# Two mixers and two expert layers in front of a second block: six PSUM banks for the first V pass, row sums in the first mixer, one U block in V

## The chip, the cores and the metric

The kernel runs as one program on one core of a Trainium2 chip. The metric is the device time of one execution in microseconds. The core has five engines that run side by side: TensorE (PE, matmuls; PEld is its weight load), VectorE (DVE), ScalarE (ACT), GpSimd (POOL) and SyncE (SP), which here only issues DMAs.

## What the reference computes

Two blocks of two layers each over 256 tokens of width 1024; the first block also carries 256 context tokens. What matters here is the first block. Each of its layers is a mixer (latent attention, a Fourier branch and a convolution, gated and merged) and then an expert layer with 16384 experts: every token picks 16 experts in each of 8 heads, and

```python
u = jnp.take(u_tab, eid, axis=0)
act = jax.nn.gelu(jnp.einsum('chkd,cd->chk', u, hc)) * gate
v = jnp.take(v_tab, eid, axis=0)
return jnp.einsum('chk,chkd->cd', act, v)
```

Shifts, scales and gates of each layer come from a conditioning row: `silu(cond) @ w_mod + b_mod`, 6 times 1024 numbers for each layer of the first block. The second block is two layers of FFN, hybrid attention, FFN, with conditioning of its own.

## The kernel before, in words

**Numbers.** Every large product is done in three matmuls (`mm3`, lines 369 to 373): weights and activations are split into a high part (rounded to float32r) and a low part, and high x high, high x low and low x high are summed in a PSUM bank. Weights arrive in pieces of 512 KB (128 x 1024, `raw`, issued on SP). `split` makes the high half on ACT (`wh`, line 339) and the low half on DVE (`wl`, line 340; with `share` set, each second or third of them on POOL). There are four `raw` buffers and two each of `wh` and `wl` in the first block's mixers and in its first expert layer.

**The order of the work.** A scheduler puts the instructions of each engine in a fixed order when the kernel is built: it takes them in the order of the program, moves ready ones ahead by simulated times, and `high_priority(300)` lets the top-k work overtake. `issue_after(x)` keeps instructions behind `x` on that engine. On the chip each engine goes through its list and waits where an input or a buffer is not there.

**The mixer** (`mixer`, line 798 on). Its last stage (lines 928 to 968) merges the three branches. For each of eight output blocks d it makes three sums in four `mm` banks, which DVE multiplies with the gates (lines 943 and 947) and splits into `m`; between these d the remaining 18 of 24 gate blocks are computed. Then `wout` is applied for eight d, and DVE adds the result to `xt` (line 961).

**The expert layer** (`peer`, line 1173 on) does not gather for most tokens: it computes all experts densely and zeroes what was not picked. In the first layer 384 of the 512 tokens go this way (nd = 384); the first 128 (g0) are done by row gathers (`rows_up`, `rows_down`), 128 rows each.

- *U stage.* 32 blocks of four steps; each step is one piece of `ut`, 24 matmuls and a Gelu. The block's result `a4` is written to DRAM (`ad`, line 1260). Between the steps `topk` advances by a budget: each of its yields has a cost, a step pays 3.05 of them in the first layer. At its end `topk` writes gate sums from one-hot matmuls (lines 1093 to 1125) to DRAM (`gd`). For the first layer the loop always runs all 32 blocks. `rows_up` advances 1.17 rows a step once the first tile's picks are there.
- *V pass.* `prep` (line 1273) loads gate sums (`g4`) and `a4` of a block, multiplies them on DVE (line 1285) and splits the product into `w4h` and `w4l`. Two blocks form a group (`deep` = 2, so 16 groups): for each of eight d, 8 x 3 matmuls of 384 columns into one `mm` bank, which DVE adds to `xt` in two instructions (line 1292). Behind each of these, `sums` advances by 0.42 steps and `rows_down` by 1.15 rows (DVE line 1170, the gathers on POOL, line 1138, four buffers).
- *Banks.* The layer has 2 `mm` banks, 3 `sc`, 1 `io` and 2 for `xg`, from its beginning to its end.
- *Bias table.* `bias_load` and `bias_write` (lines 1474 to 1498) make a table for the second block; two DMAs of 1532 KB on POOL's queue (`dd`) write it.

**Row sums** (`sums_begin`, `sums_step`, `sums`, `sums_end`, lines 420 to 468). The conditioning of later layers is not made by matmuls: each of its 128-row pieces (512 KB, `arow`) is loaded on SP into a ring and multiplied on DVE with the conditioning row, the product's sum going to one column (line 443). A step issues one load and does the product of the load before (by the ring's depth). For the second layer of the first block there are 48 pieces; the first 16 are needed for both conditioning rows, so they take two products. These 48 run in the first V pass, with a ring of four.

Of the kernel before, what the change touches and what calls it, by code (L numbers as in the profile page):

```python
# [233 lines left out]
class Kernel:  # L234
# [563 lines left out]
    def mixer(self, l):  # L798
# [6 lines left out]
        with ExitStack() as es:  # L805
# [121 lines left out]
            with self.banks(mm=4, sc=3), self.pool(f"op{l}") as op:  # L927
                m = self.t(op, [P, 2, 8, n], "m", F32R)
                v = [self.t(op, [P, 2, n], f"v{j}", F32R) for j in range(2)]
                for cc in range(2):  # L930
                    y, h, lo = st["acc"][:, cc], v[0][:, cc], v[1][:, cc]
                    nc.scalar.activation(h, y, AF.Copy, scale=0.5)
                    nc.vector.scalar_tensor_tensor(lo, y, 0.5, h.bitcast(F32), op0=OP.mult, op1=OP.subtract)
                wb = self.stream("wb", 8 * l)
                for d in range(8):
                    acc = None
                    for b, (act, k0, nk) in enumerate(((st["ao"], 0, 4), (st["f"], 4, 2), (v, 6, 2))):
                        ps = self.ps("mm")[:, :n]
                        for k in range(nk):
                            wh, wl = wb(d * 8 + k0 + k)  # L940
                            self.mm3(ps, wh, wl, act[0][:, k], act[1][:, k], k == 0, k == nk - 1)
                        t = self.t(op, [P, n], "gt" if b == 0 else "gu", bufs=2)
                        nc.vector.scalar_tensor_tensor(t, zg[3 * d + b], 1.0, ps, op0=OP.add, op1=OP.mult)
                        if acc is None:
                            acc = t
                        else:
                            nc.vector.tensor_tensor(acc, acc, t, op=OP.add)
                    nc.scalar.activation(m[:, 0, d], acc, AF.Copy, scale=0.5)
                    nc.vector.scalar_tensor_tensor(
                        m[:, 1, d], acc, 0.5, m[:, 0, d].bitcast(F32), op0=OP.mult, op1=OP.subtract  # L950
                    )
                    self.fill(f)
                    for _ in range(3):
                        i = next(gates, None)
                        if i is not None:
                            gate(i)

                def e3(d, ps):
                    for s in range(len(streams)):
                        x = self.xt[:, d, cols_of(s)]  # L960
                        nc.vector.scalar_tensor_tensor(
                            x, ps[:, cols_of(s)], mod[:, 16 + d, s : s + 1], x, op0=OP.mult, op1=OP.add
                        )
                        self.track(d, s)

                if l == 0:
                    self.need(30)
                self.linear(self.stream("wout", 8 * l), 8, range(8), (lambda k: m[:, 0, k], lambda k: m[:, 1, k]), e3, n=n)

# [8 lines left out]
    rate = {("gate", 0): (10, 0, 2), ("gate", 1): (4, 0, 2), ("u", 0): 0, ("u", 1): 0, ("v", 0): 0.42, ("v", 1): 1.25, "up": 1.17, "down": 1.15, "ffn": 1.4, "out": 1, "att": (0.4, 0.4), "norm": ((4,4), (2,2), (4,4), (4,4))}  # L978
# [194 lines left out]
    def peer(self, l, budget):  # L1173
# [8 lines left out]
        with ExitStack() as es:  # L1182
            es.enter_context(self.banks(mm=2 if g0 else 4, sc=3, io=1))
# [12 lines left out]
            with self.pool(f"tp{l}") as tp:  # L1196
# [44 lines left out]
                while nb < 32 and not (done and not g0):  # L1241
# [25 lines left out]
            if nb == 32:  # L1267
                hes.close()
            with self.pool(f"vp{l}") as vp:
# [52 lines left out]
                if l == 0:  # L1322
                    self.sums_begin(
                        vp, 4, (0, 1), self.sums_of("wmodt", 0, self.mod1[1], "b_mod1", lambda m: (0, 1) if m < 16 else (0,))
                    )
                else:
# [26 lines left out]
                self.sums_end()  # L1353
# [294 lines left out]
    def run(self):  # L1648
# [13 lines left out]
        self.peer(0, 3.05)  # L1662
# [39 lines left out]
```

## Time and profile before

| | |
|---|---|
| median of 3 runs | 4217.4 us (4212.7 to 4218.16) |
| profiled execution | 4220.82 us |
| its span, first to last instruction | 4219.0 us |
| mean granted TensorE clock | 0.946 |
| busy: PE, DVE, ACT, POOL | 3821.8, 3217.7, 1792.4, 959.9 us |
| moved by DMA | 946.53 MB, 224 GB/s |

The stages follow one another on one core: first mixer to about 490 us, first expert layer from there (U stage to 1292, V pass to 1988), second mixer to about 2256, second expert layer to about 3092, then the second block. Times of rows below are counted from the span's first instruction. A line of the profile names engine, line of the kernel, the tile written and the tiles read; the idle time of an engine stands with the instruction that it waited for, and "waits" rows give a total, a count and the longest wait in us. A table of stretches gives for each stretch its length, then busy time (and number of instructions begun) of PE, PEld, DVE, ACT and POOL, the granted TensorE clock, the share of DMA time and GB/s.

### The profile page before, as it was taken

The numbers are of one execution on the slowest core, as the hardware profiler recorded it, in microseconds if no ns is written. First come the engines' busy times: TensorE is split into PE (matmuls) and PEld (weight loads), VectorE is DVE, ScalarE is ACT, GpSimd is POOL, SyncE is SP. The second block draws the span as 40 slices with busy tenths as digits, with TensorE's granted clock in tenths as the row PEclk, the third lists the DMA queues.
The fourth block names the chain that finished last, engine by engine and source line by source line (L and its number), as shares of the span: only waits on it lengthen the run. The fifth ranks groups of instructions, "written<-read, shape, count | busy, mean of one in ns | idle before, by whom it ended". The sixth has DMA issues, their size and how long they took to land.

```text
span 4219.0 us, 69354 instructions
## 1 busy us (share of the span) xinstructions
PE 3821.8 (91%) x25443; PEld 3558.0 (84%) x25443; DVE 3217.7 (76%) x7949; ACT 1792.4 (42%) x2986; POOL 959.9 (23%) x804
## 2 busy tenths in 40 slices
PE   7889998888885789999989999999989989999898
PEld 5568798888884688888778999999989879998798
DVE  4754589999895799997758998788868768656764
ACT  3342332433442222233444656544444554444643
POOL 0100024755543233330201758100000010101100
PEclk9999999999986899999999999999999989999999
DMA  5422257898757999994325777999869429554344
GB/s 179 155 79 97 80 202 275 297 312 281 247 188 170 321 343 351 363 358 152 119 71 180 241 255 241 364 361 358 311 233 316 165 78 323 171 185 150 100 159 142
DMA packets 331412, 946.53 MB, mean 224 GB/s; under 512 B 30865, under 2 KB 118545, under 8 KB 331073
## 3 DMA queue, kind: packets, MB, share of 16 engines
q1 hardware_dynamic: 201920, 722.93, 48.8%
q0 software_dynamic: 38272, 137.38, 10.2%
q10 hardware_dynamic: 90880, 81.79, 5.8%
q8 instruction: 201, 3.29, 0.3%
q14 instruction: 139, 1.13, 0.1%
HBM read 856.01 MB, written 85.98 MB: 223 GB/s over the span
## 4 chain that ended last, share of the span: by engine, by line
PE 37%; DVE 7%; issue 7%; DMA 1%; ACT 1%; POOL 1%; ACTq 0%; POOLq 0%; DVEq 0%; SPq 0%
PE mm L371 11%; PE mm L373 11%; PE mm L372 11%; DVE wl L340 2%; DVE cj L1053 1%; PE sc L1114 1%; DMA raw<-in_vt 1%; ACT wh L339 1%; DVE cacc L770 0%; DVE nu L535 0%; PE sc L510 0%; PE sc L699 0%; PE nm L709 0%; ACTq L1260 0%; PE sc L495 0%
## 5 line engine op out<-in xcount | busy, mean ns | idle before, releaser
L339 ACT ACTIVATE wh<-raw 128x1024 fp32r<-128x1024 f32 x946 | 997.2, 1057 | 1604.9 <-PE mm L372 1254.7
L340 DVE TENSOR_TENSOR wl<-raw,wh 128x1024 fp32r<-128x1024 f32 x839 | 1043.4, 1247 | 502.8 <-ACT wh L339 492.2
L371 PE MATMUL mm<-w4h,wh 128*128 128x384 f32 (+1 forms) x2048 | 642.7, 317 | 95.0 <-DVE xt L1292 53.7
L373 PE MATMUL mm<-h2h,wl 128*128 128x256 f32 (+2 forms) x2176 | 689.3, 318 | 39.3 <-DVE wl L340 37.7
L371 PE MATMUL mm<-h2h,wh 128*128 128x256 f32 (+2 forms) x2176 | 689.4, 318 | 25.6 <-ACT a L1229 16.0
L372 PE MATMUL mm<-h2l,wh 128*128 128x256 f32 (+2 forms) x2176 | 687.6, 316 | 0.0
L373 PE MATMUL mm<-w4h,wl 128*128 128x384 f32 (+1 forms) x2048 | 620.1, 315 | 29.3 <-DVE wl L340 29.1
L372 PE MATMUL mm<-w4l,wh 128*128 128x384 f32 (+1 forms) x2048 | 637.8, 314 | 1.2 <-DVE w4l L340 1.2
L371 PE MATMUL mm<-h,wh 128*128 128x256 f32 x1712 | 499.9, 292 | 16.4 <-ACT h L540 6.7
L372 PE MATMUL mm<-h,wh 128*128 128x256 f32 x1712 | 496.1, 290 | 2.0 <-DVE h L541 1.3
L371 PEld LDWEIGHTS mm<-w4h,wh 128*128 128x128 f32 x2048 | 395.8, 194 | 115.2 <-issue 62.2
L373 PE MATMUL mm<-h,wl 128*128 128x256 f32 x1712 | 492.4, 288 | 0.5 <-DVE wl L340 0.5
L373 PEld LDWEIGHTS mm<-h2h,wl 128*128 128x128 f32 x2176 | 420.7, 193 | 50.3 <-DVE wl L340 44.6
L371 PEld LDWEIGHTS mm<-h2h,wh 128*128 128x128 f32 x2176 | 420.9, 194 | 34.1 <-ACT a L1229 19.4
L372 PEld LDWEIGHTS mm<-h2l,wh 128*128 128x128 f32 x2176 | 421.5, 194 | 2.6
L373 PEld LDWEIGHTS mm<-w4h,wl 128*128 128x128 f32 x2048 | 389.3, 194 | 34.1 <-DVE wl L340 34.0
L372 PEld LDWEIGHTS mm<-w4l,wh 128*128 128x128 f32 x2048 | 395.9, 194 | 3.2 <-DVE w4l L340 1.9
L371 PEld LDWEIGHTS mm<-h,wh 128*128 128x128 f32 x1712 | 337.0, 197 | 23.9 <-ACT h L540 10.2
L372 PEld LDWEIGHTS mm<-h,wh 128*128 128x128 f32 x1712 | 336.4, 196 | 9.3 <-DVE h L541 6.7
L340 POOL TENSOR_TENSOR wl<-raw,wh 128x1024 fp32r<-128x1024 f32 x107 | 263.2, 2460 | 352.5 <-ACT wh L339 341.0
L373 PEld LDWEIGHTS mm<-h,wl 128*128 128x128 f32 x1712 | 336.2, 197 | 0.7 <-DVE wl L340 0.7
L1121 POOL TENSOR_TENSOR stg<-s 128x256 f32<-128x256 f32 x320 | 266.8, 858 | 93.8 <-ACT s L1119 86.7
(356 smaller groups left out, 7316.2 us busy)
## 6 DMA issues: line engine op xcount, KB each, us to landing
raw<-in_ut SPq DMA_DIRECT2D x256, 512.0 KB, 4.4
raw<-in_vt SPq DMA_DIRECT2D x256, 512.0 KB, 5.8
raw<-in_wgu SPq DMA_DIRECT2D x176, 512.0 KB, 4.3
arow<-in_adat SPq DMA_DIRECT2D x144, 512.0 KB, 5.3
raw<-in_wdn SPq DMA_DIRECT2D x88, 512.0 KB, 4.3
gd<-stg ACTq DMA_DIRECT2D x20, 2048.0 KB, 13.3
raw<-in_win SPq DMA_DIRECT2D x66, 512.0 KB, 3.3
raw<-in_wmod SPq DMA_DIRECT2D x48, 512.0 KB, 4.4
```

The costliest lines, as they stand in the source:

```text
L339: self.nc.scalar.activation(h, src, AF.Copy)
L340: (eng or self.nc.vector).tensor_sub(l, src, h.bitcast(F32))
L371: mm(out, wh, xh, start=start, stop=False)
L372: mm(out, wh, xl, start=False, stop=False)
L373: mm(out, wl, xh, start=False, stop=stop)
L1053: nc.vector.scalar_tensor_tensor(junk, self.iota[:, :NCAND], pf[:, h, k : k + 1], eid[:, h, :], op0=OP.is_equal, op1=OP.mult, accum_out=se ...
L1114: nc.tensor.matmul(pg[:, j * 256 : (j + 1) * 256], oa[:, 2 * h + j], obs[h][:, j].rearrange("p a b -> p (a b)"), start=True, stop=True,)
L1121: nc.gpsimd.tensor_tensor(stg[:, :, c : c + 2].rearrange("p b t -> p t b"), both[:, :, 0], both[:, :, 1], op=OP.add)
```

## The change

- The row sums for the second layer leave the first V pass and go to the last stage of the first mixer, with a ring of two: five steps behind each of the eight d of the merge, 1.3 behind each of the eight d of `wout`, the rest at the end. The rate in V is 0 for the first layer.
- The `gu` buffer of the merge goes from two to one.
- The U loop of the first layer also ends when `topk` is done. Its budget is 3.1 instead of 3.05, `rows_up` advances 1.22 instead of 1.17. A block that U has not done is done in `prep`, as in the second layer; the order of V then begins with it. The hidden states (`hp`) are freed before V only if all 32 blocks were done in U.
- Before the first V pass the layer's banks are given back, and six `mm` and two `sc` banks are taken.

```diff
--- before.py
+++ after.py
@@ -931,6 +931,10 @@
                     y, h, lo = st["acc"][:, cc], v[0][:, cc], v[1][:, cc]
                     nc.scalar.activation(h, y, AF.Copy, scale=0.5)
                     nc.vector.scalar_tensor_tensor(lo, y, 0.5, h.bitcast(F32), op0=OP.mult, op1=OP.subtract)
+                if l == 0:
+                    self.sums_begin(
+                        op, 2, (0, 1), self.sums_of("wmodt", 0, self.mod1[1], "b_mod1", lambda m: (0, 1) if m < 16 else (0,))
+                    )
                 wb = self.stream("wb", 8 * l)
                 for d in range(8):
                     acc = None
@@ -939,17 +943,18 @@
                         for k in range(nk):
                             wh, wl = wb(d * 8 + k0 + k)
                             self.mm3(ps, wh, wl, act[0][:, k], act[1][:, k], k == 0, k == nk - 1)
-                        t = self.t(op, [P, n], "gt" if b == 0 else "gu", bufs=2)
+                        t = self.t(op, [P, n], "gt" if b == 0 else "gu", bufs=2 if b == 0 else 1)
                         nc.vector.scalar_tensor_tensor(t, zg[3 * d + b], 1.0, ps, op0=OP.add, op1=OP.mult)
                         if acc is None:
                             acc = t
                         else:
                             nc.vector.tensor_tensor(acc, acc, t, op=OP.add)
                     nc.scalar.activation(m[:, 0, d], acc, AF.Copy, scale=0.5)
-                    nc.vector.scalar_tensor_tensor(
+                    last = nc.vector.scalar_tensor_tensor(
                         m[:, 1, d], acc, 0.5, m[:, 0, d].bitcast(F32), op0=OP.mult, op1=OP.subtract
                     )
                     self.fill(f)
+                    self.sums(self.rate["mix"][0], last)
                     for _ in range(3):
                         i = next(gates, None)
                         if i is not None:
@@ -958,14 +963,17 @@
                 def e3(d, ps):
                     for s in range(len(streams)):
                         x = self.xt[:, d, cols_of(s)]
-                        nc.vector.scalar_tensor_tensor(
+                        last = nc.vector.scalar_tensor_tensor(
                             x, ps[:, cols_of(s)], mod[:, 16 + d, s : s + 1], x, op0=OP.mult, op1=OP.add
                         )
                         self.track(d, s)
+                    self.sums(self.rate["mix"][1], last)
 
                 if l == 0:
                     self.need(30)
                 self.linear(self.stream("wout", 8 * l), 8, range(8), (lambda k: m[:, 0, k], lambda k: m[:, 1, k]), e3, n=n)
+                if l == 0:
+                    self.sums_end()
 
     ratio = (1.0, 1.9)
     ahead = 4
@@ -975,7 +983,7 @@
     ratio2 = (1.0, 1.3)
     on_pool = 6
     pool_x = (0, 0, 0, 0, 0, 0, 0, 0)
-    rate = {("gate", 0): (10, 0, 2), ("gate", 1): (4, 0, 2), ("u", 0): 0, ("u", 1): 0, ("v", 0): 0.42, ("v", 1): 1.25, "up": 1.17, "down": 1.15, "ffn": 1.4, "out": 1, "att": (0.4, 0.4), "norm": ((4,4), (2,2), (4,4), (4,4))}
+    rate = {("gate", 0): (10, 0, 2), ("gate", 1): (4, 0, 2), ("u", 0): 0, ("u", 1): 0, ("v", 0): 0, ("v", 1): 1.25, "mix": (5, 1.3), "up": 1.22, "down": 1.15, "ffn": 1.4, "out": 1, "att": (0.4, 0.4), "norm": ((4,4), (2,2), (4,4), (4,4))}
 
 
     def topk(self, l, tt, tp, qT, gd, keep):
@@ -1180,7 +1188,8 @@
         gd = self.t(self.dram, [32, P, nd // 32, 4 * 32], f"gd{l}")
         ad = self.t(self.dram, [32, P, 4, nd], f"ad{l}")
         with ExitStack() as es:
-            es.enter_context(self.banks(mm=2 if g0 else 4, sc=3, io=1))
+            pes = es.enter_context(ExitStack())
+            pes.enter_context(self.banks(mm=2 if g0 else 4, sc=3, io=1))
             self.iota = self.ps("io")[:, 0:P]
             nc.scalar.activation(self.iota, self.c("iota"), AF.Copy)
             if l == 1:
@@ -1238,7 +1247,7 @@
                 tg = tk()
                 done = False
                 nb = owed = 0
-                while nb < 32 and not (done and not g0):
+                while not done and nb < 32:
                     for a4 in ublock(4 * nb):
                         owed += budget
                         while owed > 0:
@@ -1266,6 +1275,9 @@
                 self.share = 0
             if nb == 32:
                 hes.close()
+            if g0:
+                pes.close()
+                pes.enter_context(self.banks(mm=6, sc=2))
             with self.pool(f"vp{l}") as vp:
                 deep = 2 if l == 0 else 4
                 wb = 2 * deep
@@ -1319,11 +1331,7 @@
                                 op0=OP.mult, op1=OP.add,
                             )
 
-                if l == 0:
-                    self.sums_begin(
-                        vp, 4, (0, 1), self.sums_of("wmodt", 0, self.mod1[1], "b_mod1", lambda m: (0, 1) if m < 16 else (0,))
-                    )
-                else:
+                if l == 1:
                     self.sums_begin(vp, 3, (2,), self.sums_of("adat", 0, self.mod2[0], "ada_b0", lambda m: (2,)))
                 if g0:
                     acc = self.t(vp, [P, D], "racc")
@@ -1350,7 +1358,8 @@
                             self.mm3(ps[:, :nd], wh, wl, gh[:, kk], gl[:, kk], k == 0, k == 4 * deep - 1)
                         ev(d, ps[:, :nd], i + deep == 32)
                     todo = todo[deep:]
-                self.sums_end()
+                if l == 1:
+                    self.sums_end()
 
 
     def scales(self, l, j):
@@ -1659,7 +1668,7 @@
         if self.stop == "mix0":
             return self.dump()
 
-        self.peer(0, 3.05)
+        self.peer(0, 3.1)
         if self.stop == "peer0":
             return self.dump()
         self.mixer(1)
```

## Rows read from the trace of the kernel before

**Rows 1.** The page: busy time of each engine; ACT's high halves, busy and mean ns

```profile
PE 3821.8 (91%) x25443; PEld 3558.0 (84%) x25443; DVE 3217.7 (76%) x7949; ACT 1792.4 (42%) x2986; POOL 959.9 (23%) x804
...
L339 ACT ACTIVATE wh<-raw 128x1024 fp32r<-128x1024 f32 x946 | 997.2, 1057 | 1604.9 <-PE mm L372 1254.7
```

**Rows 2.** Table of stretches, columns as told above

```profile
302.00:490.00 188.00, 185.16 (x817) 152.77 (x815) 86.05 (x114) 55.55 (x78) 0.00 (x0) 1.00 0.28 93
512.00:1240.00 728.00, 655.77 (x3578) 630.56 (x3578) 640.95 (x2611) 292.62 (x454) 346.55 (x311) 0.95 0.74 254
1240.00:1292.00 52.00, 39.19 (x96) 27.00 (x96) 51.49 (x120) 28.63 (x49) 37.17 (x50) 0.52 0.58 178
...
1308.00:1400.00 92.00, 47.50 (x193) 43.10 (x194) 34.99 (x59) 15.45 (x25) 11.83 (x9) 0.69 0.99 223
1420.00:1580.00 160.00, 135.58 (x743) 129.16 (x742) 157.13 (x247) 46.12 (x63) 53.28 (x36) 0.99 0.93 341
1720.00:1880.00 160.00, 145.98 (x798) 140.02 (x797) 151.05 (x230) 49.88 (x69) 51.93 (x38) 0.98 0.95 359
...
1950.00:1988.00 38.00, 37.99 (x220) 37.67 (x218) 24.32 (x44) 14.80 (x24) 0.00 (x0) 1.00 0.37 120
2700.00:2800.00 100.00, 100.00 (x835) 99.89 (x834) 94.69 (x175) 46.50 (x71) 0.00 (x0) 1.00 1.00 382
440.00:490.00 50.00, 47.16 (x209) 38.43 (x207) 27.18 (x47) 15.98 (x28) 0.00 (x0) 1.00 0.29 96
```

**Rows 3.** Timeline of PE between the U stage and V

```profile
1308.22 1.01 PE L371 MATMUL mm<-w4h,wh 128*128 128x384 f32 x2 [16.19 <-ACT w4h L339]
```

**Rows 4.** DMA issues, 1308 to 1400 us: count, KB each, median us to landing

```profile
raw<-in_vt SPq DMA_DIRECT2D x7, 512.0 KB, 30.1
...
dd<-bv POOLq DMA_DIRECT2D x2, 1532.0 KB, 64.9
```

**Rows 5.** DMA issues, 302 to 490 us

```profile
raw<-in_win SPq DMA_DIRECT2D x14, 512.0 KB, 3.2
```

**Rows 6.** Waits, 1400 to 1935 us: total, times, longest

```profile
PE mm L371 <- DVE xt L1292: 46.4, 39, 4.0
...
PE mm L373 <- DVE wl L340: 2.6, 3, 1.6
```

**Rows 7.** DVE's groups of instructions, 1420 to 1580 us: busy, mean ns, idle before

```profile
L1292 DVE SCALAR_TENSOR_TENSOR xt<-mm,mod,xt 128x128 f32<-128x128 f32 (+1 forms) x62 | 23.0, 417 | 0.0
...
L443 DVE SCALAR_TENSOR_TENSOR cjunk<-arow,crow 128x1024 f32<-128x1024 f32 x13 | 15.9, 1222 | 0.0
L443 DVE SCALAR_TENSOR_TENSOR arow<-arow,crow 128x1024 f32<-128x1024 f32 x12 | 14.7, 1225 | 0.0
```

**Rows 8.** DVE's groups of instructions, 1720 to 1880 us

```profile
L1292 DVE SCALAR_TENSOR_TENSOR xt<-mm,mod,xt 128x128 f32<-128x128 f32 x64 | 23.7, 414 | 0.0
...
L443 DVE SCALAR_TENSOR_TENSOR arow<-arow,crow 128x1024 f32<-128x1024 f32 x13 | 15.8, 1219 | 0.0
L443 DVE DVE_READ_ACCUMULATOR arow<-arow,crow 128x1 f32 x13 | 1.1, 87 | 0.0
```

**Rows 9.** DVE's groups of instructions, 1400 to 1988 us

```profile
L1292 DVE SCALAR_TENSOR_TENSOR xt<-mm,mod,xt 128x128 f32<-128x128 f32 x240 | 88.8, 414 | 4.1 <-PE mm L373 4.1
```

**Rows 10.** SP's own waits, 1400 to 1925 us

```profile
SPq L437 <- DVE arow L443: 82.2, 43, 5.2
```

**Rows 11.** DMA issues, 1400 to 1925 us

```profile
vr<-in_vg,rowid POOLq DMA_INDIRECT x118, 7.5
```

**Rows 12.** Timeline of DVE, the merge: ends of two blocks d

```profile
331.91 0.69 DVE L949 SCALAR_TENSOR_TENSOR m<-gt,m 128x512 fp32r<-128x512 f32 x1 [0.70 <-ACT m L948]
...
353.67 0.69 DVE L949 SCALAR_TENSOR_TENSOR m<-gt,m 128x512 fp32r<-128x512 f32 x1 [0.70 <-ACT m L948]
```

**Rows 13.** The tile arow, 3100 to 3600 us: DVE idle before it, landing times

```profile
  DMA arow<-in_adat: 13.9, 20
...
DMA to landing us min/median/max: 4.1/5.1/6.0
```

## The prediction

> **What bounds the kernel now.** The page first: TensorE is busy 91% of 4219.0 us, VectorE (DVE) 76%, ScalarE (ACT) 42% [rows 1]. That is an average over stages, so the table of stretches comes next [rows 2]. Three kinds of stage touch the change.
>
> The end of the first mixer (302 to 490 us) has TensorE busy for 185 of 188 us and DVE for 86: TensorE sets the pace, DVE has 102 us to spare, and DMA moves 93 GB/s.
>
> The U stage of the first expert layer (512 to 1240) has both near 90%, and a tail (1240 to 1292) in which DVE is busy 51.5 of 52 us with top-k work while TensorE runs 96 one-hot matmuls at a granted clock of 0.52. Then TensorE stands for 16.2 us, until the gate sums have gone to DRAM and back and DVE has multiplied them in [rows 3].
>
> The first V pass over the table follows. Up to 1400 it is starved: DMA share 0.99, TensorE busy 47.5 of 92 us. Two writes of the bias table take 64.9 us to land there, and weights of 512 KB take 30.1 us where the mixer's take 3.2 [rows 4, 5]. From 1400 on DVE is the bound: 98% busy in 1420 to 1580, 94% in 1720 to 1880, and TensorE's longest wait is for DVE to empty a bank (xt, 46.4 us in 39 waits), while its waits for the weights' low halves (wl) come to 2.6 us [rows 2, 6].
>
> One group of blocks (two blocks, eight d) is 16 xt instructions. 62 of them in 160 us make 41.3 us a group; 64 in 160 make 40.0 [rows 7, 8]. All 240 after 1400 make 15 groups in 588 us [rows 9], but the last two run with the row gathers done (POOL has none from 1950 on), at TensorE's own pace: 220 recorded matmuls in 38.0 us, 0.173 us each, so 33.2 us for a group's 192 [rows 2]. The other thirteen took (588 - 2 x 33.2)/13 = 40.1 us each.
>
> **The change, step by step.** The base is the profiled execution: 4220.8 us, span 4219.0. The median of the runs is 4217.4, which is 3.4 less; that is taken off at the end.
>
> *Row sums out of V.* In 1420 to 1580 the 25 products cost DVE 15.9 + 14.7 us, 7.9 a group; in 1720 to 1880 the 13 cost 15.8, 4.0 a group [rows 7, 8]. DVE's load was 157.1/3.875 = 40.5 and 151.0/4 = 37.8 us a group [rows 2], so without them it is 32.6 to 33.8, say 33.5. TensorE needs 33.2. Both bounds of a group are now within 1% of each other.
>
> *Six banks.* The wait on xt goes as a wait of its own; what it was worth is in the group time and is not added again. What is late next is either DVE's total (33.5) or the weights' low halves. Bounds: 33.5, if neither waits for the other, as in the second layer's V pass (TensorE busy 100.0 of 100 us with DVE at 94.7); 38.1, if DVE keeps only the 0.88 share that it had in the U stage, where both also stood near 90% [rows 2]. I take 36.0, which is DVE at 0.93, its share of 1720 to 1880, nearest in place and kind. Thirteen groups by 40.1 - 36.0: **-54 us** (ends: -86 and -26).
>
> *Its DMA.* 48 loads of 512 KB and two rows leave a stage that moves 341 to 359 GB/s at a share of 0.93 to 0.95 [rows 2]. A group then moves 8 vt and some 9 vr loads of 0.52 MB and 2 + 2 blocks of 0.79 MB: 12.1 MB, 335 GB/s at 36.0 us. SP spent 82.2 us in V waiting to issue these loads, with weights queued behind [rows 10]; that wait goes too. Nothing is added for it. POOL's gathers follow DVE's pace, with four buffers and 7.5 us to land against four rows of about 3.9 us: hidden [rows 11].
>
> *The last U block in V.* With costs of 3.1 a step the code's top-k yields run out in the 122nd of 128 steps, in block 30, so one block of 96 matmuls moves (16.6 us at 0.173). If the U stage were TensorE's, all of it would be won: -17. If the block comes behind the top-k work, its four splits, matmuls and Gelu stand where the 16.2 us wait is now: about +5. Since the stage ends with DVE at 51.5 of 52 us, its end moves only by DVE's part of four splits (2 of 3 are DVE's, 1.2 us each), -3; a write and a read of 768 KB are saved, and V starts without the four row loads ahead of its blocks. I take **-4**. The two bias writes stay and starve the first group as before: 0, at best the six row loads' 3.1 MB, some -10 at 223 to 341 GB/s. The new banks lie over the top-k banks; a matmul that gets one of those waits for the last one-hot sum, which V waits for anyway: 0. Hidden states stay allocated through V, in place of the sums' ring: 0. The faster row products (1.22 a step) only come earlier in the U stage: 0. The halved gu buffer has writer and reader both on DVE: 0.
>
> *Row sums into the mixer.* 64 products of 1.3 us (with their accumulator read) are 83 us, and DVE has 102 free; two Tanh of 1.05 us fall on an ACT busy 55.6 of 188 us. The loads bring 25 MB more to 17.5 MB: 226 GB/s, below the 382 that a later stretch shows [rows 2]. SP's weight loads behind these loads wait about 1.9 us each, as in V [rows 10], with four raw buffers of 5.4 us ahead: 0. With a ring of two, two steps take a landing (3.2), an issue (0.3) and a product (1.3), so 2.4 us a step [rows 5, 8]. By the code five steps follow each of eight d. While gates are mixed in, a d lasts 21.8 us [rows 12] and they fit; in the first three d, where each step has two products, DVE's 10 us of its own (86 of 188) and 13 more fill it and some weights come late. From 440 to 490 there are 19 steps, 46 us of ring time in 50, and DVE has 27 + 25 us of work in 50 [rows 2]. Bounds: 0, if all fits; +36, with landings of 5.1 as in the first FFN (3.4 us a step, 15 us over) and 1.3 us more at each of the 16 double steps [rows 13]. I take **+8**: about 3 in the first d, 2.6 before the last d of m, 2.6 ahead of the next norm.
>
> Sum: -54 - 4 + 8 = -50; 4220.8 - 50 - 3.4 = **4167 us**.
>
> **Rivals.** *A, V runs at TensorE's pace.* Groups of 33.2: 13 x 6.9 = -90, with the other terms -86: 4131. For it: the stretch at 2700 to 2800 [rows 2]. Against it: DVE's 33.5 lies above.
> The Trainium skill's "SBUF — State Buffer" (Summary: rules for kernel authors) reckons HBM-to-SBUF transfers at about 358 GB/s. By that rule 12.1 MB need 33.8 us and A is 13 x 6.3 = -82 instead of -90. The trace doesn't hold to it: 382 GB/s over 100 us [rows 2].
>
> *B, the wait moves from the banks to the weights.* Only two wh and two wl buffers serve V. A pair of pieces is released half a d (12 matmuls, 2.1 us) before it is needed, and ACT's 1.06 plus DVE's 1.2 fill that already [rows 1]. Today the wait on xt hides it. If each of eight pieces waits 0.75 us more for a DVE that is 93% busy, a group is 39.2: -12 - 4 + 8 = -8, 4209: at the edge of no change. Against it: 2.6 us of such waits in V, and none at the end of V, where DVE is 64% busy [rows 2, 6].
>
> *C, DVE stands before late rows in the mixer: slower.* DVE takes its instructions in the order laid down; a product whose row has not landed holds the weights' halves and the emptying of banks behind it. DVE has 102 - 83 - 3 = 16 us spare (3 for the two rows' own products), so it decides from 16/48 = 0.33 us per load on. At a full landing of 3.3 us, 48 x 3.3 - 16 = +142: -54 - 4 + 142 = +84, 4301. It turns the sum positive from 1.5 us per load on. Against it: with the same ring of two in the first FFN such waits came to 13.9 us for 72 loads, 0.19 each, though landings took 5.1 us [rows 13].
> The Trainium skill's "TensorE: Matmul & The Clock Gate" (Architectural detail) calls ACT's and DVE's queues strictly first in, first out, which is C's condition; the trace agrees in that DVE idles in 20 waits there.
>
> **How the numbers follow.** The forecast with its own spread (4130 to 4198) gets 0.66, A 0.12, B 0.14, C 0.08. A measurement here tells about 0.2%, 8.4 us, from no change. Faster than 4209: the forecast, A and 0.04 of B, 0.82. Within: 0.09 of B. Slower than 4226: C and 0.01 of B, 0.09. The range runs from A, a little beyond (4125), to the edge of B (4209), and leaves out C and the outer half of B and of A.
>
> **What would show it.** Between the start of V and its end some 50 us less, groups at 36 instead of 40; DVE still at 0.9 or more there; the wait on xt below 10 us, and weights' halves (wl) the longest wait instead. In the mixer from 302 on DVE at 160 of about 195 us, TensorE nearly as busy as before. The starved stretch after the first V matmul as long as before, with two bias writes of 60 us or more. The end of top-k within 5 us of 1292 plus what the mixer adds. Wrong would be: waits of DVE for arow above 0.5 us a load in the mixer (C), groups at 39 with wl the wait (B), or a mixer longer by more than 36 us.

## The result, and the profile after

The kernel after takes **4175.7 us** (median of 4 runs, 4165.3 to 4180.7) against 4217.8 for the kernel before beside it: ratio **0.9896, 95% interval 0.9879 to 0.9913**, 42 us less by the medians and 44 between the two profiled executions. 4167 us was forecast, and the time lies inside the forecast's own spread. But two terms of the sum were wrong by some 20 us each, in opposite directions, and the total hides it. The profiled execution took 4176.9 us, with a span of 4175.2.

The table of stretches of the kernel after, with the columns of [rows 2]; the tail of the U stage now ends at 1311 instead of 1292 us:

```profile
302.00:490.00 188.00, 183.40 (x792) 149.83 (x791) 155.53 (x245) 54.42 (x74) 0.00 (x0) 0.98 0.69 225
...
512.00:1240.00 728.00, 642.87 (x3456) 615.48 (x3455) 631.49 (x2564) 278.72 (x429) 334.19 (x297) 0.94 0.73 248
1240.00:1311.00 71.00, 53.36 (x142) 37.25 (x140) 71.00 (x161) 38.17 (x65) 46.07 (x62) 0.55 0.41 126
1420.00:1580.00 160.00, 156.44 (x893) 154.05 (x892) 152.61 (x235) 54.76 (x74) 57.44 (x38) 1.00 0.94 343
1720.00:1880.00 160.00, 156.67 (x891) 153.78 (x890) 149.46 (x226) 55.86 (x77) 64.78 (x41) 1.00 0.91 327
```

The mixer (first line) now has DVE at 155.5 us instead of 86.1 and TensorE nearly as busy as before. In V (the last two lines) it is the other way round from [rows 2]: TensorE is busy 98% and DVE 93 to 95%. The wait for DVE to empty a bank, 46.4 us in [rows 6], has left the list. These are all of TensorE's waits that the view gives, 1420 to 1900 us (total, times, longest):

```profile
PE mm L373 <- DVE wl L340: 5.6, 10, 1.4
PE mm L371 <- ACT wh L339: 3.1, 11, 0.3
```

The evictions in that stretch give the length of a group of blocks: 224 of them, 16 to a group, are 14 groups in 480 us, 34.3 us each (40.1 before). From DVE's groups of instructions, 1420 to 1900 us:

```profile
L1304 DVE SCALAR_TENSOR_TENSOR xt<-mm,mod,xt 128x128 f32<-128x128 f32 x224 | 82.3, 411 | 5.5 <-PE mm L373 5.3
```

In the mixer, DVE's waits for the rows that the sums read (the tile arow; idle time before it, times):

```profile
  DMA arow<-in_wmodt: 19.6, 20
```

The loss sits between. The last one-hot matmul of the top-k starts at 1311.2 us instead of 1291.5, and the first V matmul at 1329.8 instead of 1308.2. The 19 us between these two are no longer a wait: the moved U block runs there (TensorE busy 19.0 of 19 us). V is then starved as before, until 1410 us:

```profile
1350.00:1370.00 20.00, 7.68 (x28) 7.05 (x26) 7.47 (x14) 1.93 (x4) 1.01 (x1) 0.66 0.99 81
1370.00:1390.00 20.00, 6.91 (x25) 6.45 (x24) 3.90 (x6) 1.06 (x1) 0.94 (x1) 0.74 0.99 99
1390.00:1410.00 20.00, 1.65 (x4) 1.14 (x4) 4.98 (x9) 3.82 (x6) 0.99 (x1) 0.50 0.96 305
```

By stage, before to after: the mixer ends 3.6 us later (first matmul of the row transposes, 495.3 to 498.9); the U stage from there to the last one-hot matmul is 796.2 to 812.3; from there to the first V matmul 16.7 to 18.6; V from its first matmul to its last 679.5 to 606.7; all that follows 2231.3 to 2238.7. The sum is 3.6 + 16.1 + 1.9 - 72.8 + 7.4 = -43.8 us, the difference of the spans.

All kernels that were run, by the same marks. "Mixer end" is the first matmul of the row transposes, U goes from there to the last one-hot matmul, "gap" on to the first V matmul, V to its last matmul, "rest" to the end of the span. The stages are those of one profiled execution; the median is that of all runs, and the ratio is to the kernel before, run beside it.

| kernel | median us | ratio, 95% interval | mixer end | U | gap | V | rest |
|---|---|---|---|---|---|---|---|
| before | 4217.8 | 1 | 495.3 | 796.2 | 16.7 | 679.5 | 2231.3 |
| after | 4175.7 | 0.9896 (0.9879, 0.9913) | 498.9 | 812.3 | 18.6 | 606.7 | 2238.7 |
| sums_only | 4206.9 | 0.9971 (0.9954, 0.9988) | 498.7 | 805.2 | 21.7 | 641.2 | 2227.4 |
| banks_only | 4184.3 | 0.9911 (0.9882, 0.9939) | 495.0 | 799.0 | 16.7 | 646.9 | 2233.7 |
| sums_and_banks | 4172.1 | 0.9888 (0.9856, 0.9920) | 500.8 | 798.6 | 21.7 | 611.6 | 2239.6 |
| move_old_rates | 4159.7 | 0.9860 (0.9831, 0.9890) | 497.5 | 802.3 | 18.3 | 603.8 | 2227.9 |
| old_up | 4173.0 | 0.9878 (0.9853, 0.9904) | 501.9 | 810.3 | 18.7 | 604.4 | 2237.8 |
| old_budget | 4161.5 | 0.9847 (0.9820, 0.9874) | 496.8 | 804.2 | 18.2 | 604.0 | 2241.0 |
| ad_on_pool | 4134.7 | 0.9807 (0.9791, 0.9824) | 498.1 | 775.6 | 18.3 | 606.9 | 2231.7 |
| before_ad_on_pool | 4195.3 | 0.9956 (0.9941, 0.9970) | 494.6 | 778.6 | 16.4 | 673.9 | 2226.3 |
| bias_in_mixer | 4140.7 | 0.9807 (0.9781, 0.9833) | 498.8 | 799.6 | 18.9 | 543.8 | 2274.8 |
| bias_in_attention | 4103.1 | 0.9740 (0.9719, 0.9760) | 498.4 | 795.1 | 18.3 | 542.5 | 2244.8 |
| best_old_rates | 4088.4 | 0.9699 (0.9685, 0.9713) | 505.2 | 775.4 | 18.6 | 542.4 | 2241.8 |
| best_new_rates | 4086.0 | 0.9694 (0.9678, 0.9709) | 498.0 | 772.9 | 18.0 | 543.2 | 2250.9 |

The last column tells how far one profile can be trusted: in the ten kernels that leave everything behind V as it was (the first ten rows), it goes from 2226 to 2241 us. The 7.4 us of the rest in the kernel after lie within that and are put down to nothing. U scatters too: in the six kernels with the sums in the mixer, the budget of 3.05 and the stores of the U blocks on ACT it goes from 795.1 to 805.2 us, so a few us there say nothing.

### The profile page after: what moved, and what is told of

It is laid out like the page before. It is cut to its first block, busy times and chain, and to the rows that moved or that the text cites. A ratio compares the mean times of both kernels' runs of the same rounds, so it can differ in the third digit from the quotient of the medians.

```text
span 4175.2 us, 69284 instructions
## 1 busy us (share of the span) xinstructions
PE 3820.4 (92%) x25443; PEld 3562.4 (85%) x25443; DVE 3235.8 (77%) x7950; ACT 1794.7 (43%) x2986; POOL 968.9 (23%) x803
## 4 chain that ended last, share of the span: by engine, by line
PE 46%; DVE 8%; issue 7%; DMA 3%; ACT 1%; POOL 1%; another core or an unknown queue 1%; ACTq 0%; SPq 0%; DVEq 0%; POOLq 0%
PE mm L373 14%; PE mm L371 14%; PE mm L372 14%; DVE wl L340 2%; DMA raw<-in_vt 2%; DVE cj L1061 1%; ACT wh L339 1%; PE sc L1122 1%; DMA arow<-in_adat 1%; DMA gd<-stg 1%; DVE cacc L770 1%; DVE w4l L340 0%; DVE nu L535 0%; PE sc L510 0%
## 5 line engine op out<-in xcount | busy, mean ns | idle before, releaser
L340 DVE TENSOR_TENSOR wl<-raw,wh 128x1024 fp32r<-128x1024 f32 x840 | 1054.6, 1259 | 446.4 <-ACT wh L339 439.2
L371 PE MATMUL mm<-h2h,wh 128*128 128x256 f32 (+2 forms) x2176 | 692.7, 320 | 20.7 <-ACT a L1238 13.8
L371 PE MATMUL mm<-w4h,wh 128*128 128x384 f32 (+1 forms) x2048 | 631.8, 312 | 26.0 <-ACT wh L339 25.8
L373 PE MATMUL mm<-w4h,wl 128*128 128x384 f32 (+1 forms) x2048 | 601.2, 312 | 35.2 <-DVE wl L340 35.1
L371 PE MATMUL mm<-h,wh 128*128 128x256 f32 x1712 | 498.4, 291 | 16.5 <-ACT h L540 6.7
L371 PEld LDWEIGHTS mm<-h,wh 128*128 128x128 f32 x1712 | 335.5, 196 | 24.2 <-ACT h L540 10.4
L1146 POOL DMA_INDIRECT vr<-in_vg,rowid x128 | 196.0, 1531 | 375.3 <-DVE racc L1178 350.6
```

What stands on the lines that cost most here:

```text
L340: (eng or self.nc.vector).tensor_sub(l, src, h.bitcast(F32))
L371: mm(out, wh, xh, start=start, stop=False)
L373: mm(out, wl, xh, start=False, stop=stop)
L1146: self.nc.gpsimd.indirect_dma_start(out=r, out_offset=None, in_=self.A[table], in_offset=bass.IndirectOffsetOnAxis(ap=ids[:, i : i + 1], a ...
```

## The experiments

**Which part of the change made V shorter?** The kernel before, with the sums moved and nothing else; with the six banks and nothing else; and with both.

```
sums_only:       before, plus, in the mixer (and the same for e3, with [1]; the ring's end behind wout;
                 one gu buffer and the rates "mix" (5, 1.3) and ("v", 0) 0 as in the kernel after),
+                if l == 0:
+                    self.sums_begin(op, 2, (0, 1), ...)
+                    self.sums(self.rate["mix"][0], last)
                 and in V
-                if l == 0:
-                    self.sums_begin(vp, 4, (0, 1), ...)
banks_only:      before, plus
+            if g0:
+                pes.close()
+                pes.enter_context(self.banks(mm=6, sc=2))
sums_and_banks:  both; the loop still runs all 32 U blocks; 3.05 and 1.17 as before
```

> The kernel before with one part of the change: the row sums in the first mixer, none in V; two matmul banks in V, all 32 U blocks, the old rates. Theory D (DVE's load was V's bound): groups go from 40.1 to about 36 us, V is 54 us shorter, the mixer 4 longer, 4168 us. Rival T (TensorE is held by having two banks, whatever DVE's load): groups stay above 38 us, V at most 27 us shorter, about 4195 us, with xt still TensorE's longest wait.

> The kernel before with another part: six matmul banks in the first V pass, the row sums still in V, all 32 U blocks, the old rates. Theory D: DVE is busy 37.8 to 40.5 us a group in V, so a group can't fall under that; V is 0 to 30 us shorter, 4190 to 4218 us, DVE at 97% or more. Rival T: TensorE no longer waits for a bank, groups at 36 us or less, 4165 us or less.

> Both of these parts, with all 32 U blocks and the old rates. Both theories: V about 65 us shorter, as in the kernel after. What differs is the stretch ahead of V: if the 15 us that the U stage lost come from the moved block or its rates, top-k ends near 1296 us, the 16 us gap is there again, and the time is 4156 to 4162 us, below the kernel after. If they come from the new place of the sums (a shifted order of work in U), top-k ends near 1311, the gap comes on top, and the time is near 4172 to 4180 us.

In V the sums alone are worth 38.3 us, the banks alone 32.6, both together 67.9: nearly the two added (70.9). Neither theory held whole. With the sums gone and two banks left, a group takes 36.9 us (208 evictions in 480 us). TensorE still waits longest for a bank (its waits, 1420 to 1900 us: total, times, longest):

```profile
PE mm L371 <- DVE xt L1301: 23.9, 14, 2.9
```

And DVE, although it has less to do, stands idle for ACT's weight halves, 43.4 us in the same stretch (its groups: busy, mean ns, idle time before):

```profile
L340 DVE TENSOR_TENSOR wl<-raw,wh 128x1024 fp32r<-128x1024 f32 x104 | 127.0, 1221 | 43.5 <-ACT wh L339 43.4
```

The rows can be read as a loop: a matmul that waits for a bank holds its weights longer, ACT's next halves wait for their buffers, DVE waits for ACT, and then DVE is late with the next bank. No run takes the links of that loop apart. In the kernel after, the same idle time in front of wl is 13.0 us. With six banks and the sums still in V, DVE fills every gap, and a group is 37.3 us (206 evictions). The stretches 1500 to 1700 and 1700 to 1900 us of banks_only:

```profile
1500.00:1700.00 200.00, 185.76 (x1018) 174.69 (x1016) 199.92 (x319) 61.12 (x82) 66.14 (x43) 1.00 0.96 359
1700.00:1900.00 200.00, 192.54 (x1075) 185.26 (x1075) 199.48 (x313) 67.25 (x93) 66.95 (x47) 1.00 0.97 364
```

DVE at 99.9% is a bound, and theory D drew it too high: it took DVE's load of before, and with six banks the load of a group fell. The products of the row gathers lie otherwise in the order that was laid down: 108 of them beside 206 evictions, 8.4 a group, where the kernel before has 111 beside 192, 9.25 a group. One takes 1.28 us in both (before, then banks_only, 1420 to 1900 us):

```profile
L1170 DVE SCALAR_TENSOR_TENSOR racc<-vr,rowdot,racc 128x1024 f32<-128x1024 f32 x111 | 142.5, 1284 | 0.3
L1170 DVE SCALAR_TENSOR_TENSOR racc<-vr,rowdot,racc 128x1024 f32<-128x1024 f32 x108 | 138.0, 1278 | 0.0
```

That is 1.1 of the 2.7 us by which a group became shorter (40.0 to 37.3), so the banks' gain is in part a lower load, and not only fewer waits. What TensorE waits for longest in that stretch is now the weights' low halves, rival B's wait:

```profile
PE mm L373 <- DVE wl L340: 17.4, 26, 2.2
```

sums_only gains 38 us in V and much less in all: 25 in the profiled execution, 11 by the median (its runs go from 4195.1 to 4220.7, and the profiled one is among the shortest). It pays 3.4 in the mixer, 9 in the U stage and 5 in the gap. sums_and_banks, with the same U code, pays 5.5, 2.4 and 5. The gap's 5 us, which both have, stay unexplained. sums_and_banks fits neither of its two forecasts whole: top-k ends at 1299.4 us, near the 1296 of the first, but the time is that of the second, with the longer gap and a rest 8 us longer than before.

**Where did the U stage lose its 16 us?** The moved block or one of the two rates.

```
move_old_rates:  after, with
-        self.peer(0, 3.1)          +        self.peer(0, 3.05)
-  "up": 1.22                       +  "up": 1.17
old_up:          after, with "up": 1.17 alone
old_budget:      after, with 3.05 alone
```

> The kernel after with the two rates of before (budget 3.05 in place of 3.1, row products 1.17 in place of 1.22 a step); the last U block still runs in V. If the rates cost the U stage its 15 us: top-k ends near 1296 us, V starts near 1313, about 4160 us. If it is the moved block itself: top-k ends near 1311 and the time is within 5 us of the kernel after, 4171 to 4181 us.

> The kernel after with 1.17 row products a step in place of 1.22; the top-k budget stays at 3.1. With both rates old, top-k ended at 1299.8 us in place of 1311.2 and the time was 4159.7 in place of 4175.7 us. If the faster row products are to blame (a product and its gather more in each twenty steps on a DVE that is 90% busy): 4160 us, top-k's end near 1300. If it is the budget: 4176 us, end near 1311. If neither has a cause of its own (a laid-down order that came out differently, with one 13.6 us stall of ACT in issuing a store near 890 us): both single returns lie between, with stalls of their own at other places.

> The kernel after with a budget of 3.05 in place of 3.1; the row products stay at 1.22 a step. If the budget is to blame (more top-k work per U step early, so less U work beside it later): 4160 us, top-k's end near 1300. If the row products are: 4176 us, near 1311. If the order alone: in between, or above both.

The moved block is not to blame: with the old rates the block still moves, U is 802.3 us, inside the scatter above, and the time 4159.7. Against sums_and_banks the profile has 3.4 us less in the gap and 7.8 less in V (by the medians 12 us less in all, though the two intervals overlap). The budget is to blame: with 3.05 alone U is 804.2 and the time 4161.5; with the row products alone put back, 810.3 and 4173.0, and the runs of the two do not overlap (4152.5 to 4166.0, and 4169.0 to 4174.9). What goes with the larger budget is seen on ACT. From ACT's timeline in the kernel after (start, length, idle time before; ACTq is a DMA that ACT issues):

```profile
887.34 0.38 ACTq L1133 DMA_DIRECT2D gd<-stg  x1
887.82 0.60 ACT L1001 ACTIVATE s<-sc 128x512 f32<-128x512 f32 x1 [1.94 <-POOL stg L1129]
...
889.27 13.65 ACTq L1269 DMA_DIRECT2D ad<-a  x1
902.96 1.57 ACT L1001 ACTIVATE s<-sc 128x512 f32<-128x512 f32 x3 [12.78 <-issue]
```

And from DVE's:

```profile
903.59 1.06 DVE L1006 MAX8 top<-s 128x8 f32<-128x128 f32 x5 [10.46 <-ACT s L1001]
```

A U block's store (ad), which takes ACT 0.33 us in most cases, is issued 1.9 us behind a gate-sum store (gd) of 2 MB and holds ACT for 13.65 us. The next token tile's scores wait behind it, and DVE stands 10.5 us: the start of the next top-k has nothing to work on. old_up has the same stall, 13.84 us, at the same place of the code. In move_old_rates all four of these copies come before the store (ACT's timeline):

```profile
891.70 0.38 ACTq L1133 DMA_DIRECT2D gd<-stg  x1
892.12 1.58 ACT L1001 ACTIVATE s<-sc 128x512 f32<-128x512 f32 x3 [1.35 <-POOL stg L1129]
...
896.31 0.59 ACT L1001 ACTIVATE s<-sc 128x512 f32<-128x512 f32 x1
...
901.47 2.99 ACTq L1269 DMA_DIRECT2D ad<-a  x1
```

It has more such stalls in sum (6.2, 3.0, 9.0 and 5.7 us against 4.0, 13.7 and 0.8), but DVE's longest wait for scores is 4.6 us there. DVE's waits for scores in U, 520 to 1300 us, in the kernel after and in move_old_rates (total, times, longest):

```profile
DVE top L1006 <- ACT s L1001: 20.1, 4, 10.5
DVE top L1006 <- ACT s L1001: 11.8, 3, 4.6
```

These 8.3 us are most of the 10.0 by which U differs between the two kernels.

**Is it the stall, or the order that the budget gives?** The stores from another queue.

```
ad_on_pool, before_ad_on_pool:
-                    nc.scalar.dma_start(ad[nb], a4)
+                    nc.gpsimd.dma_start(ad[nb], a4)
```

> The kernel after, rates 3.1 and 1.22 as they are, with the stores of the U blocks (ad) issued by POOL in place of ACT. Theory: with the new budget one such store is issued 2 us behind a gate-sum store of 2 MB on ACT's queue and holds ACT 13.65 us; ACT's copies of the scores come late, DVE waits 10.5 us for them, and top-k ends 11 us later. With the store on another queue ACT doesn't stand, top-k ends near 1300 in place of 1311 us, and the time is 4158 to 4168 us. Rival: the order of work that the larger budget gives is worse by itself (the stall only sits in it), or POOL now stands for Gelu and its row gathers come late: 4172 us or more, with top-k's end at 1308 or later.

> The kernel before with one edit: the stores of the U blocks issued by POOL in place of ACT. In the kernel before ACT stood 9.6 and 5.5 us in two such stores that came 2 to 10 us behind a gate-sum store. In the kernel after, the same edit moved top-k's end from 1311.2 to 1273.7 us, 37.5 where the stalls summed to 17.6. If ACT's standing in these stores (and what waits behind it) is lost time in any U stage: top-k ends 10 to 30 us earlier than 1291.5, 4190 to 4208 us. If it hurt only where the new budget put it: within 5 us of 4218.

U falls to 775.6 us in the one and 778.6 in the other; 4134.7 and 4195.3 us. POOL spends 0.6 us on each of these issues. So these stores on ACT cost the U stage of both kernels. The theory came out right in direction and too small: it gave U 11 us and the time 8 to 18, and the gain is 37 and 41 in the kernel after. The stalls' sum doesn't tell the gain either: before has 33 us of them (9.6, 5.5, 10.4, 7.9) and gains 18, after has 18 and gains 37. It matters what stands behind each, and the order of the instructions is laid down anew with every such edit; how much of the 37 is the one stall and how much the order was not separated.

The stall can't be all of it. In the U stage of the kernel after DVE stood idle 97.6 us and here 80.0, which is 18 less; but it was also busy 714.7 us and here 695.6, which is 19 less, and 14 of these 19 are the same 91 splits of weights (the kernel after, then ad_on_pool, each over its own U stage):

```profile
L340 DVE TENSOR_TENSOR wl<-raw,wh 128x1024 fp32r<-128x1024 f32 x91 | 131.0, 1440 | 38.3 <-ACT wh L339 34.2 <-PE sc L1122 3.7
L340 DVE TENSOR_TENSOR wl<-raw,wh 128x1024 fp32r<-128x1024 f32 x91 | 117.4, 1290 | 28.8 <-ACT wh L339 28.6
```

Seventeen of them take more than 1.4 us in the kernel after and nine here, where 1.22 is usual, and POOL is at work during every one of these. The longest, from the timelines of DVE and POOL in the kernel after:

```profile
1095.90 5.31 DVE L340 TENSOR_TENSOR wl<-raw,wh 128x1024 fp32r<-128x1024 f32 x1
1095.03 2.38 POOL L340 TENSOR_TENSOR wl<-raw,wh 128x1024 fp32r<-128x1024 f32 x1
1097.35 2.77 POOL L1129 TENSOR_TENSOR stg<-s 128x256 f32<-128x256 f32 x4
```

So the order of work also decides which splits fall beside POOL's work; that POOL is what lengthens them was not tested. In the kernel before, the same edit leaves DVE's busy time as it was (704.3 and 703.8 us) and takes 17 us of its idle time.

The Trainium skill's "DMA: Bandwidth & Descriptors" (Issuing engines are not separate DMA queues) says that starting transfers from several engines only saves the sequencer's time of starting them, which it calls usually small beside the transfer. The rows differ in the size: that time was 13.65 us here, on an engine that had other work behind it.

**What is the starved stretch worth?** The prediction left it as it was. The two writes of the bias table go into the second layer's mixer: at its start, or behind the first softmax of its attention, where DMA stood nearly still for some 60 us (0 to 2 GB/s from 2050 to 2110 us in move_old_rates). The small loads of their sources (0.4 MB) move with them. Both with the old rates.

```
-                bias = self.bias_load(vp) if l == 0 else None
-                    if l == 0 and i == 8:
-                        self.bias_write(vp, *bias)
in both, at the mixer's beginning:
+                bias = self.bias_load(ap) if l == 1 else None
bias_in_mixer, ahead of the second mixer's interleave(main(), ...):
+                if l == 1:
+                    self.bias_write(ap, *bias)
bias_in_attention, in main(), behind the first softmax (self.late is a copy on ACT there; the loop around is cut):
+                            if l == 1 and i == 0:
+                                with self.tc.issue_after(self.late.ins):
+                                    self.bias_write(ap, *bias)
```

> The kernel after with both old rates, and the load of the bias table's sources and its two writes to DRAM taken out of the first V pass and put into the second layer's mixer, where DMA's share is 0.3 to 0.45. Theory: these two writes alone starve the first V group; 16 groups at TensorE's 33.5 us are 536 us where the pass took 603.8, so V gets 45 to 60 us shorter, the mixer 0 to 15 longer: 4100 to 4130 us. Rival: the first group is late from its own loads of weights, gates and stored products, which must all come at once after the gate sums' round trip; then V gains 15 us or less and the time is 4145 us or more.

> The kernel after with both old rates, and the bias table's two writes issued in the attention part of the second layer's mixer, behind its first softmax, where DMA moved 0 to 5 GB/s for some 70 us. Issued in front of that mixer, the same writes left V 60 us shorter but starved the mixer's first weights (TensorE 14.4 of 50 us busy): 4140.7 us. Theory: two writes of 33 us fit into the idle stretch, V keeps its gain, the mixer loses 0 to 8 us: 4098 to 4110 us. Rival: the weights behind the attention, loaded during it, come late by what the writes reach past it: 4115 to 4135 us.

V falls from 603.8 to 543.8 and 542.5 us: so it is these two writes that starve its first groups; 0.4 MB of loads can't account for 60 us at the 372 to 396 GB/s below. Where the kernel after had TensorE at 8 of 20 us, bias_in_mixer has:

```profile
1340.00:1360.00 20.00, 19.67 (x114) 19.35 (x113) 20.00 (x34) 8.18 (x13) 9.99 (x4) 1.00 1.01 372
1360.00:1380.00 20.00, 18.62 (x102) 17.23 (x101) 20.00 (x33) 6.22 (x9) 7.11 (x5) 1.00 1.01 396
...
1900.00:1950.00 50.00, 14.35 (x72) 13.01 (x70) 3.97 (x6) 5.08 (x8) 0.71 (x1) 0.60 0.95 98
```

The last line is the price at the new place: issued at 1883 us, they starve the mixer's weights instead, DMA's share at 0.95 for 98 GB/s, and the rest is 2274.8 us, 34 above the longest of the first ten. The theory had given the mixer 0 to 15 us more and 4130 us at most; the time is 4140.7. Behind the softmax the same two writes take 61 us to land, with nothing else to move, and TensorE goes on:

```profile
2000.00:2050.00 50.00, 40.92 (x217) 26.59 (x215) 24.11 (x70) 21.65 (x51) 0.71 (x1) 0.90 0.95 54
```

**Both gains together**, with either pair of rates:

```
best_old_rates: bias_in_attention plus nc.gpsimd.dma_start(ad[nb], a4)
best_new_rates: the same with peer(0, 3.1) and "up": 1.22
```

> The kernel after with the bias table's writes in the second mixer's attention, the U blocks' stores issued by POOL, and both old rates (3.05 and 1.17). Theory: the two gains add up, as they lie in different stages: 4103 less 10 to 28 us (by what the stores cost at the old rates), 4075 to 4093 us. Rival: at the old rates ACT's stalls were hidden, nothing is gained: 4098 to 4108 us.

> The same with the rates of the kernel after (3.1 and 1.22). Theory: 4134.7 us with the stores moved, less the 57 us that the writes' new place was worth: 4074 to 4082 us, the same as or below the old rates, so the larger budget is no loss by itself. Rival: the larger budget costs about 12 us wherever ACT's stores are issued: 12 us above the kernel with the old rates.

4088.4 and 4086.0 us: some 130 us below the kernel before and 90 below the kernel after, and no difference between the budgets (their intervals nearly coincide). With the stores on POOL, U is 772.9 to 778.6 us in all four kernels, at either budget. So the larger budget costs nothing that shows once ACT issues no such stores. Against the forecast of 4074 to 4082 the new rates miss by 4 us: their rest is 2250.9 us, the longest but for bias_in_mixer. The three kernels with the writes in the attention have rests of 2241.8 to 2250.9, against 2226 to 2241: on average the new place costs 12 us.

## Why the prediction was right, and where it was wrong

- **Row sums out of V and six banks: -54, measured -72.8.** Half of the mechanism held: DVE's load fell to TensorE's and below, and the wait on xt went. The mis-sized term is the 36.0 us a group, measured 34.3. The share taken for DVE, 0.93, came out (0.95 and 0.93), though the row that it was taken from says 0.94 (151.05 of 160). The load did not: 33.5 us forecast, 152.6/160 and 149.5/160 of 34.3 = 32.7 and 32.0 found. In the old order it would have held (sums_only: DVE busy 434.7 us in 13 groups, 33.4 each); the six banks spread the gather products, 122 beside 14 groups instead of 121 beside 13, and the working had no such term. At 98% busy TensorE is the bound, which is rival A's mechanism for V and not DVE's pace that the forecast took; the group lies between the forecast's 36.0 and A's 33.2. "It is not added again" was right of the sum of two parts, but it hid that the banks were half of it: without them the same step gives 38.3.
- **The last U block, -4, measured +18 (16.1 in U and 1.9 in the gap).** This is the step that failed, by 22 us, and in it two sentences: the budget was read only for the step in which the top-k yields run out, and the stage's end was to move "only by DVE's part of four splits". At equal rates the move does not change the U stage's end (1299.4 and 1299.8 us) and seems worth 12 us by the medians, more than forecast, but the intervals overlap. DVE had three splits fewer in U, as said (91 for 94); they took 131.0 us instead of 123.6 all the same. And a budget is also the order of work in all 122 steps: the new order put a store that ACT issues in front of the scores that DVE waits for, and 10 of the 16 us went with it. ACT's DMA issues were not in the working at all. The other 6 us are in move_old_rates too and lie within U's scatter.
- **Row sums into the mixer, +8, measured +3.6.** DVE had 155.5 of 188 us to do, where 160 of 195 were named, and its waits for rows came to 19.6 us for 48 loads: 0.41 each, below the 0.5 that would have shown rival C but above the 0.33 from which, by the prediction's own sum, it decides: 19.6 less the 16 to spare are the 3.6 us measured. TensorE stayed busy 183.4 of 188 us, so that this is the cause is not shown. In the other kernels with the sums there the mixer ends 1.5 to 9.9 us later. C at its full size, 142 us, is out.
- **Rival B** is out: waits for the low halves are TensorE's longest in V, as forecast, but 5.6 us in all. They are 17.4 us where DVE has no time left (banks_only).
- **The two bias writes, 0 in the change, 60 us left lying.** Right as a term ("starve the first group as before"), and the largest thing that the profile offered.
- The total came out 9 us above the forecast. In the profiled executions the span fell by 43.8 us instead of 50: +22 in U, -19 in V, -4 in the mixer and +7 in the rest, for which the sum had nothing. That errors of 20 us cancelled was luck. The upper end of the forecast's spread, 4198, doesn't follow from its own ends either: -26 - 4 + 8 gives 4195.

## What to carry to other kernels

An engine that computes and also issues stores is a queue like any other: count its issues, look for one right behind a large store, and ask what stands behind it; the cheapest edit of this study (one word) gave 41 us, and 21 in the kernel before. When two engines hand buffers to each other at nearly the same load, more buffers between them and less load on one are two gains to try apart: here each was worth a similar amount in V, 32.6 and 38.3 us, and the buffers changed the order of work as well. Before tuning a stage's inside, read what the DMA is doing where it starts: a slow write with nobody waiting for it cost V 60 us, and a stretch with an idle DMA was some 700 us further on.

## What was not expected of the hardware

- **A DMA issue can hold its engine.** In the ten kernels that issue the U blocks' stores on ACT, 276 of 314 take ACT 0.33 to 0.35 us. The other 38 are just those that start 0.5 to 10.2 us behind the start of a 2 MB gate-sum store on ACT, and they hold it for 0.8 to 13.8 us; the nearest of the 276 starts 10.8 us behind one. The distance alone does not give the time: at 1.4 to 2.0 us it goes from 6.0 to 13.8 us. SP has it too: in the starved stretch of the kernel after, single loads of weights and of a stored block hold it 6.3 to 6.6 us each (rows below, from SP's timeline), where 0.33 is usual; with the bias writes elsewhere no issue of SP between 1300 and 1420 us lasts over 2 us.

```profile
1363.57 6.34 SPq L344 DMA_DIRECT2D raw<-in_vt  x1
1370.01 6.41 SPq L1293 DMA_DIRECT2D a<-ad  x1
1376.51 6.63 SPq L344 DMA_DIRECT2D raw<-in_vt  x1
```

The Trainium skill's "Perfetto Trace Analysis" (DMA Instruction — HWDGE (DVE, Sync)) tells of a DMA that an engine issues in this way, and counts into such a time the wait for the descriptor generator and the generating, not the moving of the data. The rows agree that it isn't the data's time alone: 768 KB take 0.33 us to issue in most cases. Which of the two it was here, no run shows.

- **A slow write takes all of the DMA.** Two writes of 1.5 MB, alone, keep the mean share at 0.95 and move 54 GB/s (bias_in_attention, 2000 to 2050 us), where V at nearly the same share, 0.94, moves 343. Why, was not tried; a write of another shape would tell.
